# Intermediate stores moved to GpSimd's queue, and the opening's loads and first feature tile put in another order

## The chip, the cores and the metric
One core of one Trainium2 chip runs the whole program. The metric is the device time of one execution in microseconds. The engines are named as in the profile: PE (TensorE), DVE (VectorE), ACT (ScalarE), POOL (GpSimd) and SP (SyncE, which here only issues DMAs; its issue rows are marked SPq).

## The reference
Two layers of a trunk over 512 latent tokens and 256 context tokens of width 1024. Cut to what matters:
```python
for i in range(2):
    mod_l = silu(c) @ w_ada[i] + b_ada[i]          # shift, scale, gate
    mod_c = silu(c_ctx) @ w_ada[i] + b_ada[i]
    h_l = x * (1 + sc_l) + sh_l                    # 512 x 1024
    h_c = cx * (1 + sc_c) + sh_c                   # 256 x 1024
    parts = split(h @ w_in)                        # SSD | MLA | retention, with gates
    ssd = rms_norm(scan(conv5(xbc), softplus(dt + bias)) * silu(z))
    mla = softmax(q k^T) v * silu(gate)            # 8 heads, low-rank q and kv
    ret = head_norm(scan(q, k, v)) * silu(gate)    # 4 heads
    x = layer_norm(ALPHA * x + g * (concat(ssd, mla, ret) @ w_out))
return x                                           # latents only
```
Context tokens read only context; the scans run in both directions. All is fp32.

## The kernel before
Features lie on the 128 partitions and the 768 tokens on the columns: 0 to 255 context, 256 to 767 latent. Each fp32 product is done as three matmuls of split operands (`mm3`: hi with hi, hi with lo, lo with hi). `split` makes the parts: ScalarE casts hi, VectorE subtracts it for lo. So each weight tile costs a load (`wr`), a cast (`wh`) and a subtraction (`wl`) before TensorE can use it; `wslot` takes the common slots, two for `wr`, three each for `wh` and `wl`. `pslot` is the same in a slot of a stage's own pool.

`load` is a DMA from SyncE's queue, and before the change every DMA goes through it, stores as well. Much is stored to DRAM and loaded again later, often in another layout: the decay sums (`cum`, from the tile `ct`, back as `cf`), the convolved x (`xs`), the scan's outputs (`y`), MLA's inputs and operands (`cq`, `ckv`, `g`, `qh`, `kn`, `v`), retention's (`rq`, `rk`, `rv`, `rg`), the mixer's outputs (`m`), and both residual streams (`a`, `x`).

`start` is the opening. Sixteen tiles of the modulation weights (`ar`, in pairs k and k+8 for shift and scale of feature tile k) give matmuls `pr`; ScalarE copies the result (`rows`), TensorE turns it (`pm`), VectorE adds the bias (`mod`). `make_h0` loads feature tile k of x, scales and shifts it in place and splits it (`hh`, `hl`). Three weight tiles (one of 48 columns, which holds dt, and two of the convolution's inputs B and C) are then multiplied with it: matmuls `p` (latent columns) and `c` (context), 18 for each k, summed over the eight k.

Then the dt stage: `ms` is copied out, transposed (`pt`), goes through a softplus written out on VectorE, and ends in the cumulative sums `ct`, stored as `cum`. The tile `ct` shares its two buffers with `cv`, the result of the convolution, so the first convolutions (`cv<-xpad,cw`) must wait until the two stores of `cum` have read them. Behind that come the convolutions, the SSD scan with other projections (`pj`) put in between as filler, retention, MLA, and the output projection. In MLA a pair of heads ends with a chain through DRAM (`mla_head`): the denominators `den` are stored (`dd`), loaded again spread over 128 partitions (`dc`), inverted on VectorE, stored (`de`), loaded as broadcast rows (`den`), and multiplied with `num`; `den` has one buffer. This happens three times in each layer.

The order on each engine is fixed before the run by a scheduler that goes by the order of the code and by priorities (`high_priority`, which `wslot` asks for from its seventh tile on). Every engine executes in its order.

Of the kernel before, what the change touches and what calls it, by code (L numbers as in the profile page):

```python
# [18 lines left out]
KD = 8  # L19
NCTX = 256  # L20
# [68 lines left out]
class Trunk:  # L89
# [7 lines left out]
    def load(self, out, in_):  # L97
        return self.nc.sync.dma_start(out=out, in_=in_)

    def mm(self, out, lhsT, rhs, start=True, stop=True, **k):  # L100
        return self.nc.tensor.matmul(out, lhsT=lhsT, rhs=rhs, start=start, stop=stop, **k)  # L101
# [54 lines left out]

    def pslot(self, P, src, n):
        raw = P.tile([128, 1024], F32, tag="pwr", name="pwr", bufs=1)
        self.load(raw[:, :n], src)
        hi = P.tile([128, 1024], F32R, tag="pwh", name="pwh", bufs=1)  # L160
        lo = P.tile([128, 1024], F32R, tag="pwl", name="pwl", bufs=1)
        self.split(hi[:, :n], lo[:, :n], raw[:, :n])
        return hi, lo
# [40 lines left out]
    def store(self, dst, ps, gate=False):  # L204
        with self.tc.high_priority():
            st = self.sp.tile([128, T], F32, tag="st", name="st", bufs=3)
            for src, a, b in ps:
                if gate:
                    self.act(st[:, a:b], src, AF.Tanh, scale=0.5)
                    self.stt(st[:, a:b], st[:, a:b], 1.0, src, ALU.add, ALU.mult)  # L210
                else:
                    self.copy(st[:, a:b], src)
            self.load(dst[:, ps[-1][1]:T], st[:, ps[-1][1]:T])

# [93 lines left out]
    def start(self, P):  # L308

        tiles = ((M_T, 48), (B_T, 128), (B_T + 2, 128))  # L310
        lat = [self.acc.tile([128, 512], F32, tag="acc", name="p0") for _ in tiles]
        cx = [self.ps("cx", "c0", 3) for _ in tiles]
        ws = []
        for k in range(KD):
            for j in (0, 1) if k == 0 else (k + 1,):
                if j < KD:
                    self.ada(0, (j, j + 8), P)
            self.make_h0(P, k)
            if not ws:
                for t, m in tiles:  # L320
                    ws.append([x[:, :8 * m].rearrange("p (k c) -> p k c", k=8)
                               for x in self.wslot(self.A["win"][0, t][:, :8 * m], 8 * m)])
            for ps, a, b in ((lat, NCTX, T), (cx, 0, NCTX)):
                for p, (hi, lo), (t, m) in zip(ps, ws, tiles):
                    self.mm3(p[:m, 0:b - a], [(hi[:, k, :], lo[:, k, :], self.hh[k][:, a:b], self.hl[k][:, a:b])],
                             k == 0, k == KD - 1)
        self.first = []
        for pl, pc, (t, m) in zip(lat, cx, tiles):
            st = self.sp.tile([128, T], F32, tag="st", name="c0s", bufs=3)
            self.copy(st[:m, 0:NCTX], pc[:m, 0:NCTX])  # L330
            self.first.append([(pl[:m], NCTX, T), (st[:m, 0:NCTX], 0, NCTX)])
# [99 lines left out]
    def dt_stage(self):  # L431
# [26 lines left out]
        self.load(D["kr"], ms[0:32, :])  # L458
        pt = self.ps("tr", "pt", 2)
# [49 lines left out]
        for d, m in ((0, self.mf), (1, self.mb)):  # L509
            pa = self.ps("tr", "pa", 2)  # L510
            pb = self.ps("tr", "pb", 2)
            for c in range(NCH):
                o = pa[0:16, c * 128:(c + 1) * 128] if c < 4 else pb[0:16, (c - 4) * 128:(c - 3) * 128]
                self.mm(o, la[:, d, c, :], m)
            ct = S.tile([16, T], F32, tag="cv", name="ct", bufs=2)
            self.copy(ct[:, 0:512], pa[0:16, :])
            self.copy(ct[:, 512:T], pb[0:16, 0:256])
            self.load(D["cum"][d].rearrange("c h i -> h c i"), ct.rearrange("h (c i) -> h c i", i=128))
        self.cw = S.tile([128, 72], F32, name="cw")
# [31 lines left out]
    def xbc(self, g):  # L551
        nc, S, l, D = self.nc, self.S, self.l, self.D
        self.uB = S.tile([128, XC], F32, name="uB")
        self.uC = S.tile([128, XC], F32, name="uC")
        self.conv(B_T + g, self.uB)
        self.conv(B_T + 2 + g, self.uC)
        self.bt = S.tile([128, NCH, 128], F32, name="bt")
        self.xt = S.tile([128, NCH, 512], F32, name="xt")
        self.trans(self.uB, self.bt)
        for t in range(4):  # L560
            u = self.conv(X_T + g * 4 + t)
            if self.ctx:
                self.load(D["xs"][g * 4 + t][:, 0:NCTX], u[:, 0:NCTX])
            self.load(D["xs"][g * 4 + t][:, NCTX:T], u[:, 260:XC])
            self.trans(u, self.xt[:, :, t * 128:(t + 1) * 128])
# [41 lines left out]
    def ssd_y(self, c, g, hf, hb):  # L607
# [49 lines left out]
        self.tt(yv, cv[hs[0][0]], py, ALU.add)  # L657
        self.load(D["y"][g][:, :, c * 128:(c + 1) * 128].rearrange("t p i -> p t i"), ys)


    def ret_v(self):
        l = self.l
        for n in range(2):
            sl = [self.wslot(self.A["win"][l, RV_T + n * 2 + j]) for j in range(2)]
            sl = [(a.rearrange("p (k c) -> p k c", k=4), b.rearrange("p (k c) -> p k c", k=4)) for a, b in sl]
            for c in range(NCH):
# [4 lines left out]
                with self.tc.high_priority():  # L671
# [9 lines left out]
                    self.load(self.D["rv"][:, c, n * 256:(n + 1) * 256], st)  # L681

# [144 lines left out]
    def ret_y(self, P, c0, q, kk, v, Dm, ef, hs):  # L827
# [44 lines left out]
        for s in range(2):  # L872
# [6 lines left out]
            for pr in range(2):  # L879
                self.load(D["m"][4 + pr * 2 + s][:, cs], gt[:, s, pr])  # L880


    def mla_prep(self, P):
# [46 lines left out]
        nc.vector.tensor_copy(ko[:, 0:NCTX], kr[:, 0:NCTX])  # L930
        self.load(D["krr"], ko)

# [4 lines left out]
        for p in range(4):  # L937
            st = P.tile([128, T], F32, tag="st", name="st", bufs=2)
            for a, b in ((NCTX, T), (0, NCTX)):
# [4 lines left out]
                self.tt(st[:, a:b], ps[:, 0:b - a], krb[:, a:b], ALU.mult)  # L944
            self.load(D["kn"][p], st)
        wvh, wvl = v3(wv[0], 2), v3(wv[1], 2)
        for c in range(NCH):
# [4 lines left out]
            self.act(st, ps, AF.Copy, scale=ky[:, c:c + 1])  # L952
            self.load(D["v"][:, c, :], st)

        qh, ql, qrb, _ = normed(D["cq"], 3, P_QN, 384, ctx)
        bl = ([(0, NCTX)] if ctx else []) + [(NCTX, T)]
        for s in (2, 0, 1):
            w = self.pslot(P, self.A["wuq"][l, s], 768)
            wh, wl = v3(w[0][:, 0:768], 3), v3(w[1][:, 0:768], 3)
            for j in range(2):  # L960
# [13 lines left out]
                if ti < 4:  # L974
                    for s2 in range(2):
                        self.load(D["qh"][ti * 2 + s2][0:64, lo:], st[64 * s2:64 * s2 + 64, lo:])
                else:
                    for s2 in range(4):
                        self.load(D["qh"][(ti - 4) * 4 + s2][64:96, lo:], st[32 * s2:32 * s2 + 32, lo:])

# [62 lines left out]
    def mla_head(self, P, h):  # L1043
# [47 lines left out]
        self.load(D["m"][p][:, lo:], num[:, lo:])  # L1091

# [46 lines left out]
    def out_s(self, t):  # L1139
# [11 lines left out]
        else:  # L1151
# [4 lines left out]
            self.stt(x[:, lo:], x[:, lo:], self.ag[:, 8 + t:9 + t], y[:, lo:], ALU.add, ALU.add)  # L1156
        self.load(self.D["a"][t][:, lo:], x[:, lo:])

# [87 lines left out]
    def ln(self, P, X, a, b, qsum, xsum):  # L1246
# [32 lines left out]
        for t in range(8):  # L1279
# [5 lines left out]
            if a >= NCTX:  # L1285

                self.load(D["x"][t][:, a:b], X[t])
        if a >= NCTX:
            rr = P.tile([1, NLAT], F32, name="rr")
            self.copy(rr, pb[0:1, :])  # L1290
            self.load(self.rrd, rr)

# [90 lines left out]
```

## Time and profile before

| | |
|---|---|
| median of 3 runs | 1487.89 us (1486.96 to 1489.88) |
| the profiled execution | 1487.2 us, its span 1485.4 us |
| mean granted clock of TensorE | 0.982 |
| busy share of the span | PE 95%, DVE 73%, ACT 47%, POOL 2% |
| instructions of GpSimd | 31, none of them a DMA |
| DMA | 225.66 MB, 152 GB/s in the mean |

The span runs from the first to the last instruction that the profiler recorded; the rest of an execution lies around it. Times in the trace count from the span's start. The busy share of PE is an average over stages in which different things limit, and matmuls overlap in a pipeline, so a PE that is busy is not always at its peak.

### The profile page before, as it was taken

The numbers are of one execution on the slowest core, as the hardware profiler recorded it, in microseconds if no ns is written. First come the engines' busy times: TensorE is split into PE (matmuls) and PEld (weight loads), VectorE is DVE, ScalarE is ACT, GpSimd is POOL, SyncE is SP. The second block draws the span as 40 slices with busy tenths as digits, with TensorE's granted clock in tenths as the row PEclk, the third lists the DMA queues.
The fourth block names the chain that finished last, engine by engine and source line by source line (L and its number), as shares of the span: only waits on it lengthen the run. The fifth ranks groups of instructions, "written<-read, shape, count | busy, mean of one in ns | idle before, by whom it ended". The sixth has DMA issues, their size and how long they took to land. (4 is left out here: it accounts for less than half of the span.)

```text
span 1485.4 us, 23355 instructions
## 1 busy us (share of the span) xinstructions
PE 1418.2 (95%) x8660; PEld 1158.9 (78%) x8660; DVE 1084.7 (73%) x2132; ACT 693.0 (47%) x1376; POOL 22.5 (2%) x31
## 2 busy tenths in 40 slices
PE   6999999999999999999999799999999999989996
PEld 4787789778888878777788688789878887767665
DVE  3599894995485657678745858998697678678858
ACT  2346743662232434477721245565363335347743
POOL 0000000000000001000001000000000000000010
PEclk9999999999999999999999899999999999999998
DMA  8336543457724746724242222353257455563241
GB/s 335 137 101 178 184 171 107 158 183 256 256 72 157 254 160 182 240 65 137 89 156 71 91 88 87 129 135 114 86 171 226 173 188 189 196 202 98 67 128 57
DMA packets 110155, 225.66 MB, mean 152 GB/s; under 512 B 13581, under 2 KB 42381, under 8 KB 109786
## 3 DMA queue, kind: packets, MB, share of 16 engines
q1 hardware_dynamic: 110042, 224.17, 46.2%
q8 instruction: 68, 1.11, 0.3%
q14 instruction: 45, 0.37, 0.1%
HBM read 173.93 MB, written 50.20 MB: 151 GB/s over the span
## 5 line engine op out<-in xcount | busy, mean ns | idle before, releaser
L101 PE MATMUL pj<-hh,wh 128*128 128x512 f32 (+1 forms) x984 | 354.6, 361 | 2.0 <-ACT hh L115 1.6
L101 PE MATMUL pj<-hh,wl 128*128 128x512 f32 (+1 forms) x984 | 352.7, 359 | 0.0
L101 PE MATMUL pj<-hl,wh 128*128 128x512 f32 (+1 forms) x984 | 349.9, 356 | 0.0
L122 ACT CAST wh<-wr 128x1024 fp32r<-128x1024 f32 (+1 forms) x116 | 120.3, 1039 | 207.1 <-PE pj L101 94.0
L101 PEld LDWEIGHTS pj<-hh,wh 128*128 128x128 f32 x984 | 186.7, 190 | 34.0 <-issue 9.3
L101 PEld LDWEIGHTS pj<-hh,wl 128*128 128x128 f32 x984 | 186.4, 190 | 29.4 <-issue 7.0
L101 PEld LDWEIGHTS pj<-hl,wh 128*128 128x128 f32 x984 | 186.7, 190 | 29.0 <-issue 6.4
L104 DVE TENSOR_TENSOR wl<-wr,wh 128x1024 fp32r<-128x1024 f32 (+1 forms) x116 | 142.4, 1227 | 75.8 <-ACT wh L122 75.0
L104 DVE TENSOR_TENSOR pel<-pe,peh 128x512 fp32r<-128x512 f32 (+1 forms) x112 | 71.6, 648 | 35.8 <-ACT peh L115 35.3
L107 DVE SCALAR_TENSOR_TENSOR cv<-xpad,cw,cv 128x772 f32<-128x772 f32 (+1 forms) x96 | 92.2, 994 | 0.2
L115 ACT ACTIVATE pe<-psc 128x512 f32<-128x512 f32 (+1 forms) x112 | 63.7, 569 | 55.6 <-PE psc L101 46.7
L1035 DVE TENSOR_REDUCE nm<-pmx 128x1 fp32r<-128x768 f32 (+1 forms) x80 | 67.6, 845 | 15.8 <-PE pmx L101 14.6
L101 PE MATMUL po<-sh,wh 128*128 128x512 f32 (+1 forms) x192 | 69.4, 364 | 4.2 <-DVE oy L107 4.2
L101 PE MATMUL po<-sl,wh 128*128 128x512 f32 (+1 forms) x192 | 69.5, 363 | 1.7 <-DVE sl L107 1.7
L115 ACT ACTIVATE ce<-cf 64x512 f32<-64x512 f32 (+1 forms) x80 | 46.9, 586 | 49.6 <-DMA cf<-cum 48.9
L101 PE MATMUL po<-sh,wl 128*128 128x512 f32 (+1 forms) x192 | 68.9, 360 | 0.0
L115 ACT ACTIVATE tm<-sf,dt 128x128 f32<-128x128 f32 x160 | 52.5, 390 | 30.2 <-DVE sf L104 30.2
L115 ACT ACTIVATE peh<-psc 128x512 fp32r<-128x512 f32 (+1 forms) x112 | 63.6, 568 | 0.2
L115 ACT ACTIVATE arg<-arg,ncb 128x128 f32<-128x128 f32 x160 | 54.9, 393 | 4.2 <-DVE arg L107 3.8
L101 PE MATMUL pv<-wl,hh 128*128 128x256 f32 x192 | 54.7, 285 | 0.3 <-DVE wl L104 0.3
L101 PE MATMUL po<-mr,wh 128*128 128x256 f32 (+1 forms) x216 | 54.8, 339 | 0.0
L101 PE MATMUL pv<-wh,hl 128*128 128x256 f32 x192 | 54.5, 284 | 0.0
(330 smaller groups left out, 2952.2 us busy)
## 6 DMA issues: line engine op xcount, KB each, us to landing
wr<-in_win SPq DMA_DIRECT2D x82, 512.0 KB, 3.8
ar<-in_wada SPq DMA_DIRECT2D x48, 512.0 KB, 7.0
cf<-cum SPq DMA_DIRECT2D x80, 256.0 KB, 4.6
wr<-in_wout SPq DMA_DIRECT2D x32, 512.0 KB, 4.0
y<-ys SPq DMA_DIRECT2D x20, 256.0 KB, 2.6
xs<-th SPq DMA_DIRECT2D x16, 256.0 KB, 2.1
x<-in_xT SPq DMA_DIRECT2D x8, 384.0 KB, 8.7
rv<-stv SPq DMA_DIRECT2D x24, 128.0 KB, 2.6
```

Of the source, the lines that this page charges most:

```text
L101: return self.nc.tensor.matmul(out, lhsT=lhsT, rhs=rhs, start=start, stop=stop, **k)
L104: return self.nc.vector.tensor_tensor(out, a, b, op=op)
L107: return self.nc.vector.scalar_tensor_tensor(out, in0=a, scalar=s, in1=b, op0=op0, op1=op1)
L115: return self.nc.scalar.activation(out, in_, f, **k)
L122: self.nc.scalar.copy(hi, raw)
L1035: nc.vector.tensor_reduce(nm[:, i:i + 1], p1[:, 0:n], axis=AX.X, op=ALU.max, negate=True)
```

## The change
Two things are edited. A new helper `save` issues a DMA from GpSimd's queue, and 231 stores use it in place of `load`; the final stores of `out` and all loads stay on SyncE's. And `start` is written in another order: for the first feature tile the modulation pair 0, then x, then the three weight tiles, of which the small one takes a slot of its own through `pslot`; only then the pair for the next feature tile, and from there on always one pair ahead.
```diff
+    def save(self, out, in_):
+        return self.nc.gpsimd.dma_start(out=out, in_=in_)
...
-    def pslot(self, P, src, n):
-        raw = P.tile([128, 1024], F32, tag="pwr", name="pwr", bufs=1)
+    def pslot(self, P, src, n, size=1024):
+        raw = P.tile([128, size], F32, tag="pwr", name="pwr", bufs=1)
...
         for k in range(KD):
-            for j in (0, 1) if k == 0 else (k + 1,):
-                if j < KD:
-                    self.ada(0, (j, j + 8), P)
-            self.make_h0(P, k)
-            if not ws:
+            if k == 0:
+                self.ada(0, (0, 8), P)
+                self.make_h0(P, 0)
                 for t, m in tiles:
-                    ws.append([x[:, :8 * m].rearrange("p (k c) -> p k c", k=8)
-                               for x in self.wslot(self.A["win"][0, t][:, :8 * m], 8 * m)])
+                    w = (self.wslot(self.A["win"][0, t]) if m == 128 else
+                         self.pslot(P, self.A["win"][0, t][:, :8 * m], 8 * m, 8 * m))
+                    ws.append([x[:, :8 * m].rearrange("p (k c) -> p k c", k=8) for x in w])
+            if k + 1 < KD:
+                self.ada(0, (k + 1, k + 9), P)
+            if k:
+                self.make_h0(P, k)
...
-            self.load(D["cum"][d].rearrange("c h i -> h c i"), ct.rearrange("h (c i) -> h c i", i=128))
+            self.save(D["cum"][d].rearrange("c h i -> h c i"), ct.rearrange("h (c i) -> h c i", i=128))
...
-            self.load(d1[i:i + 1, :], den[64 * i:64 * i + 1, lo:])
+            self.save(d1[i:i + 1, :], den[64 * i:64 * i + 1, lo:])
...
-        self.load(fl(d2), dc)
+        self.save(fl(d2), dc)
```
The other stores are edited in the same way.

Three places show what this does to the engines' orders. The first is SyncE's queue at the start of the program, behind three small loads of constants (`ar` are modulation weights, `x` feature tiles, `wr` and `pwr` the projection's weights; `x2` and the like is a count).
```order
+L98 DMA ar<-in_wada 128x1024 x2
+L98 DMA x_144<-in_xT 128x768
+L98 DMA pwr<-in_win 128x384
+L98 DMA wr<-in_win 128x1024 x2
 L98 DMA ar<-in_wada 128x1024 x4
-L98 DMA x_171<-in_xT 128x768
-L98 DMA wr<-in_win 128x384
-L98 DMA wr<-in_win 128x1024
-L98 DMA ar<-in_wada 128x1024
-L98 DMA wr<-in_win 128x1024
-L98 DMA ar<-in_wada 128x1024
 L98 DMA x_240<-in_xT 128x768
```

The first feature tile and the weights now stand behind two modulation tiles instead of four, and the second weight tile of full size no longer behind a later `ar`.

The second is TensorE at the end of the opening. Before, behind the next-to-last projections of the last feature tile:
```order
L101 MATMUL c_116<-hl_7_104,wh 128x256
L101 MATMUL c_116<-hh_7_96,wl 128x256
L462 MATMUL pt<-K,ms 128x48 x6
L101 MATMUL pj<-hh_0_89,wh 128x512
L101 MATMUL pj<-hl_0_97,wh 128x512
L101 MATMUL pj<-hh_0_89,wh 128x256
```

and after, where these rows begin one `pj` behind the opening's last matmul `c`:
```order
L105 MATMUL pj<-hl_0_97,wh 128x512
L105 MATMUL pj<-hh_0_89,wl 128x512
L105 MATMUL pj<-hh_1_90,wh 128x512
L105 MATMUL pj<-hl_1_98,wh 128x512
L105 MATMUL pj<-hh_1_90,wl 128x512
L105 MATMUL pj<-hh_2_91,wh 128x512
L105 MATMUL pj<-hl_2_99,wh 128x512
L105 MATMUL pj<-hh_2_91,wl 128x512
L105 MATMUL pj<-hh_3_92,wh 128x512
L105 MATMUL pj<-hl_3_100,wh 128x512
L105 MATMUL pj<-hh_3_92,wl 128x512
L469 MATMUL pt<-K,ms 128x48 x6
```

Twelve projection matmuls `pj`, counting the one ahead of these rows, now stand between the opening and the six transposes `pt`, which stood ahead of all of them.

The third is GpSimd from its last constant at the program's start on, after the change:
```order
L1378 MEMSET const-uint8-127 128x1
L1386 UNCONDITIONAL_BRANCH
L102 DMA kr_557<-ms 32x768
L102 DMA cum_558<-ct 16x6x128 x2
L102 DMA xs_0_559<-th 128x256
L102 DMA xs_0_559<-th 128x512
L102 DMA xs_0_560<-th 128x256
L102 DMA xs_0_560<-th 128x512
L102 DMA rk_0_580<-st 128x768
```

Before, none of these stores stands there: they stand in SyncE's order, among the loads.

## Rows read from the trace of the kernel before

**Rows 1.** The page, part 1: busy us, share of the span, instructions.
```profile
PE 1418.2 (95%) x8660; PEld 1158.9 (78%) x8660; DVE 1084.7 (73%) x2132; ACT 693.0 (47%) x1376; POOL 22.5 (2%) x31
```

**Rows 2.** Waits of PE: us in total, times, longest us.
```profile
PE ptr L572 <- DVE th L107: 3.2, 2, 1.7
...
PE pq L101 <- ACT stv L115: 1.7, 1, 1.7
...
PE pvv L101 <- ACT stv L115: 1.3, 1, 1.3
```

**Rows 3.** Windows: length, busy us by engine, PEclk (granted clock), DMA share, GB/s.
```profile
17.00:45.00 28.00, 26.49 (x256) 19.31 (x254) 12.32 (x25) 6.28 (x10) 0.00 (x0) 0.94 1.01 393
60.00:62.00 2.00, 2.00 (x7) 1.49 (x6) 1.97 (x5) 0.08 (x2) 0.00 (x0) 0.50 0.26 76
76.00:232.00 156.00, 154.30 (x1049) 129.58 (x1048) 144.77 (x266) 90.65 (x212) 0.00 (x0) 1.00 0.50 157
```

**Rows 4.** Timeline of the opening: start us, us, engine, instruction, idle before.
```profile
6.92 1.08 PE L101 MATMUL pr<-ar,sil 128*32 128x128 f32 x16 [6.92 <-DMA ar<-in_wada]
...
10.64 0.35 DVE L112 TENSOR_SCALAR mod<-pm,pc 128x2 f32<-128x2 f32 x2 [6.12 <-PE pm L101]
...
13.81 0.86 DVE L112 TENSOR_SCALAR x<-x,mod 128x512 f32<-128x512 f32 x2
...
15.59 0.66 PE L101 MATMUL p<-hh,wh 128*48 128x512 f32 x1 [2.08 <-ACT hh L122]
...
25.48 1.25 PE L101 MATMUL p<-hh,wh 128*48 128x512 f32 x3 [0.97 <-ACT hh L122]
...
30.32 0.85 PE L101 MATMUL pr<-ar,sil 128*32 128x128 f32 x22
```

**Rows 5.** Timeline of the opening, SyncE's DMA issues (SPq).
```profile
6.23 0.57 SPq L98 DMA_DIRECT2D ar<-in_wada  x1
15.16 0.33 SPq L98 DMA_DIRECT2D wr<-in_win  x1
```

**Rows 6.** Timeline of PE at the opening's end.
```profile
58.23 0.57 PE L462 MATMUL pt<-K,ms 48*128 48x48 f32 x6 [1.60 <-ACT ms L118]
59.17 0.50 PE L101 MATMUL pj<-hh,wh 128*128 128x512 f32 x1 [0.38 <-ACT wh L122]
59.51 0.39 PE L101 MATMUL pj<-hl,wh 128*128 128x512 f32 x1
59.74 0.28 PE L101 MATMUL pj<-hh,wh 128*128 128x256 f32 x1
```

**Rows 7.** Waits in 76 to 232 us, of VectorE.
```profile
DVE wl L104 <- ACT wh L122: 5.2, 5, 2.7
```

**Rows 8.** Timeline, 74 to 77 us: the store of cum, and the first convolution.
```profile
74.30 2.20 SPq L98 DMA_DIRECT2D cum<-ct  x2
...
76.17 0.68 DVE L112 TENSOR_SCALAR cv<-xpad,cw 128x772 f32<-128x772 f32 x1 [2.00 <-ACT ct L118]
```

**Rows 9.** Timeline, 1355 to 1367 us: one chain of MLA's denominators.
```profile
1355.58 0.64 SPq L98 DMA_DIRECT2D dc<-dd  x1
...
1359.73 0.19 DVE L1085 RECIPROCAL dc<-dc 128x8 f32<-128x8 f32 x1
...
1361.38 1.10 SPq L98 DMA_DIRECT2D den<-de  x2
...
1366.16 0.68 DVE L107 SCALAR_TENSOR_TENSOR num<-num,den 128x512 f32<-128x512 f32 x1
```

**Rows 10.** DMA issues: count, KB each, median us from issue to landing.
```profile
v<-stv SPq DMA_DIRECT2D x12, 256.0 KB, 5.9
...
den<-de SPq DMA_DIRECT2D x6, 128.0 KB, 2.8
...
dc<-dd SPq DMA_DIRECT2D x3, 4.0 KB, 3.1
```

**Rows 11.** GpSimd's dearest group: busy us, mean ns.
```profile
L1214 POOL TENSOR_TENSOR lxs<-lxs,la 128x512 f32<-128x512 f32 x4 | 6.0, 1508 | 12.8 <-issue 10.3 <-DVE la L107 2.4
```

More of the change, by code (lines that the diff above doesn't have):

```diff
@@ L155, in wslot @@
         return hi, lo
-    def pslot(self, P, src, n):
-        raw = P.tile([128, 1024], F32, tag="pwr", name="pwr", bufs=1)
+    def pslot(self, P, src, n, size=1024):
+        raw = P.tile([128, size], F32, tag="pwr", name="pwr", bufs=1)
         self.load(raw[:, :n], src)
-        hi = P.tile([128, 1024], F32R, tag="pwh", name="pwh", bufs=1)
-        lo = P.tile([128, 1024], F32R, tag="pwl", name="pwl", bufs=1)
+        hi = P.tile([128, size], F32R, tag="pwh", name="pwh", bufs=1)
+        lo = P.tile([128, size], F32R, tag="pwl", name="pwl", bufs=1)
         self.split(hi[:, :n], lo[:, :n], raw[:, :n])
@@ L212, in store @@
                     self.copy(st[:, a:b], src)
-            self.load(dst[:, ps[-1][1]:T], st[:, ps[-1][1]:T])
+            self.save(dst[:, ps[-1][1]:T], st[:, ps[-1][1]:T])
     def run(self):
@@ L457, in dt_stage @@
                 self.padded[t] = self.pad(self.pre[t])
-        self.load(D["kr"], ms[0:32, :])
+        self.save(D["kr"], ms[0:32, :])
         pt = self.ps("tr", "pt", 2)
@@ L562, in xbc @@
             if self.ctx:
-                self.load(D["xs"][g * 4 + t][:, 0:NCTX], u[:, 0:NCTX])
-            self.load(D["xs"][g * 4 + t][:, NCTX:T], u[:, 260:XC])
+                self.save(D["xs"][g * 4 + t][:, 0:NCTX], u[:, 0:NCTX])
+            self.save(D["xs"][g * 4 + t][:, NCTX:T], u[:, 260:XC])
             self.trans(u, self.xt[:, :, t * 128:(t + 1) * 128])
@@ L657, in ssd_y @@
         self.tt(yv, cv[hs[0][0]], py, ALU.add)
-        self.load(D["y"][g][:, :, c * 128:(c + 1) * 128].rearrange("t p i -> p t i"), ys)
+        self.save(D["y"][g][:, :, c * 128:(c + 1) * 128].rearrange("t p i -> p t i"), ys)
     def ret_v(self):
@@ L680, in ret_v @@
                                  bias=vm[:, h:h + 1])
-                    self.load(self.D["rv"][:, c, n * 256:(n + 1) * 256], st)
+                    self.save(self.D["rv"][:, c, n * 256:(n + 1) * 256], st)
     def blocks(self):
@@ L879, in ret_y @@
             for pr in range(2):
-                self.load(D["m"][4 + pr * 2 + s][:, cs], gt[:, s, pr])
+                self.save(D["m"][4 + pr * 2 + s][:, cs], gt[:, s, pr])
     def mla_prep(self, P):
@@ L930, in mla_prep @@
         nc.vector.tensor_copy(ko[:, 0:NCTX], kr[:, 0:NCTX])
-        self.load(D["krr"], ko)
+        self.save(D["krr"], ko)
         wk = self.pslot(P, self.A["wukv"][l, 0], 1024)
@@ L944, in mla_prep @@
                 self.tt(st[:, a:b], ps[:, 0:b - a], krb[:, a:b], ALU.mult)
-            self.load(D["kn"][p], st)
+            self.save(D["kn"][p], st)
         wvh, wvl = v3(wv[0], 2), v3(wv[1], 2)
@@ L952, in mla_prep @@
             self.act(st, ps, AF.Copy, scale=ky[:, c:c + 1])
-            self.load(D["v"][:, c, :], st)
+            self.save(D["v"][:, c, :], st)
         qh, ql, qrb, _ = normed(D["cq"], 3, P_QN, 384, ctx)
@@ L975, in mla_prep @@
                     for s2 in range(2):
-                        self.load(D["qh"][ti * 2 + s2][0:64, lo:], st[64 * s2:64 * s2 + 64, lo:])
+                        self.save(D["qh"][ti * 2 + s2][0:64, lo:], st[64 * s2:64 * s2 + 64, lo:])
                 else:
                     for s2 in range(4):
-                        self.load(D["qh"][(ti - 4) * 4 + s2][64:96, lo:], st[32 * s2:32 * s2 + 32, lo:])
+                        self.save(D["qh"][(ti - 4) * 4 + s2][64:96, lo:], st[32 * s2:32 * s2 + 32, lo:])
     def mla(self, P):
@@ L1090, in mla_head @@
         self.tt(num[:, lo:], num[:, lo:], gt[:, lo:], ALU.mult)
-        self.load(D["m"][p][:, lo:], num[:, lo:])
+        self.save(D["m"][p][:, lo:], num[:, lo:])
     def mla_last(self, P):
@@ L1156, in out_s @@
             self.stt(x[:, lo:], x[:, lo:], self.ag[:, 8 + t:9 + t], y[:, lo:], ALU.add, ALU.add)
-        self.load(self.D["a"][t][:, lo:], x[:, lo:])
+        self.save(self.D["a"][t][:, lo:], x[:, lo:])
     def out_m(self, R, P):
@@ L1285, in ln @@
             if a >= NCTX:
-                self.load(D["x"][t][:, a:b], X[t])
+                self.save(D["x"][t][:, a:b], X[t])
         if a >= NCTX:
@@ L1290, in ln @@
             self.copy(rr, pb[0:1, :])
-            self.load(self.rrd, rr)
+            self.save(self.rrd, rr)
 INS = ["xT", "cT", "wada", "win", "wuq", "wukv", "wout", "pc", "cpack", "rope"]
```

## The prediction
> **What bounds the kernel now.** I read the page first. TensorE is busy for 95% of the span [rows 1], so whatever moves the end must shorten its idle time or its slow-clock time. The waits by engine then say where the idle time has a releaser, and of those that this change can reach there are few: transposes that wait for VectorE (3.2 us), and two projections of the MLA preparation that wait for ScalarE's staging tile stv (1.7 and 1.3) [rows 2]. None names a store. The windows give the stages [rows 3]: in 17 to 45 us the DMA engines are full (share 1.01, 393 GB/s); in 76 to 232 us TensorE has 154.30 of 156 us and VectorE 144.77, so there two engines are nearly full at once, and an engine that runs ahead gains only if the other follows. The reader is to see three places: the opening, its end at 56 to 60 us, and the long stage behind it.
>
> **The opening.** In it the first projection of feature tile 0 starts at 15.59 us, although the first modulation weights fed TensorE at 6.92 [rows 4]. What lies between is order: VectorE has the scale of feature tile 0 ready at 10.64 + 0.35, but the two products with x come at 13.81, behind the second pair of modulation columns; from there through ScalarE's hi cast to the matmul it is 1.78. SyncE's rows show the second fault: after its load at 6.23 it issues nothing until 15.16, because the third weight tile finds no free slot and waits for VectorE's split [rows 5]; that is a hole in the loads of 8.4 us less what was still in flight.
>
> After the change VectorE's product with x stands right behind the first modulation. Worked out: 10.99 us (mod done), if x0 has landed. It is fifth behind the two modulation tiles now: two of 512 KB and one of 384 KB are 1.44 MB, 3.7 us at the 393 GB/s of that window [rows 3]; the first tile fed TensorE at 6.92, so x0 lands about 2.3 us later, 9.3. Then the same 1.78: first projection at 12.8, **2.8 us earlier**.
>
> For feature tile 1 two things must be there. The loads in the new order up to x1 are 192 KB + 2 x 512 KB (weights), 4 x 512 KB and 384 KB, 3.74 MB or 9.5 us at that rate: 9.3 + 9.5 = 18.8. TensorE must do 18 matmuls of tile 0 (25.48 to 30.32 for those of tile 1 [rows 4]: 4.84), 64 modulation matmuls (16 took 1.08 at 6.92, right after idling; 64 would be 4.3 at that pace and 2.2 at twice it; I take 2.2, since TensorE will not have idled just before, and 0.9 for the handovers through ScalarE): 12.8 + 4.84 + 2.2 + 0.9 = 20.7. The later one counts. Then the scale, 0.35, the 1.78 again and a handover of 0.3: 23.1 against 25.48, **2.4 us earlier** (bounds 0.8 and 2.8). From there on the pace per tile is TensorE's own, before as after, so the opening ends 2.4 us earlier.
>
> **Its end.** Before, TensorE then idled 1.60 us until ScalarE had copied ms for the transposes pt, and 0.38 for the weight cast [rows 6], and the granted clock in 60 to 62 us was 0.50, its lower level (1.2 GHz), after that idling [rows 3]. In the changed order twelve pj matmuls stand between the last opening projection and pt, and their weight tile is split early, since the opening now holds only two of the common slots. So 2.0 us go, and, if the clock does not fall, also half of its low stretch: 1.0 for these two us, and 1.7 if it lasts half as long again and more. Together 2.0 to 3.7. TensorE enters the next stage **4.4 to 6.1 us ahead**.
>
> **What VectorE lets through.** It is the other full engine there. Its start on the convolutions does not move by as much: pt comes only 1.2 us earlier (2.4 and the gap of 1.60, less twelve matmuls at 0.23, from one start at 59.51 to the next at 59.74 [rows 6]), the softplus chain behind it is VectorE's own work, and the first convolution reuses the tile ct, so it waits until cum is stored: SyncE issues that at 74.30, and VectorE starts at 76.17, having waited 2.00 [rows 8]. This store moves to GpSimd. What a store costs from there no row shows, since GpSimd issues none now. Nearest rows from both sides: SyncE's issue of one transfer takes 0.33 [rows 5]; GpSimd's own dearest instruction 1.51 [rows 11]. Call the extra delay of a stored result d. From below it is 0 or less, for the stv stores take 5.9 us to land behind loads on SyncE's queue where dd to dc takes 3.1 [rows 10], so another queue can also help; from above I take 2, a little over GpSimd's row. I use **d = 1**, between, nearer GpSimd's own rows as it is GpSimd that works. So VectorE starts its convolutions at the same time as before (1.2 earlier, 1 later).
>
> VectorE gains in that stage only where it waited for TensorE or ScalarE behind TensorE: 5.2 us for the weights' hi casts [rows 7], which wait for slots that TensorE frees; with smaller waits besides I take 6 as the bound. Against it, the changed order puts some five more projection matmuls, 1.2 to 1.4 us, ahead of the places where TensorE needs VectorE. From the lead of 4.4 to 6.1, less those matmuls and under this bound, I take **4 us** gained at 232 (bounds 0 and 6). The transposes' wait for th [rows 2], up to 1.7 at once and one of the two at the end of this stage, shows that VectorE, not TensorE, decides there; that is why I don't pass on the whole lead.
>
> **The other 228 stores.** (231 less the three of the stage above, kr and cum.) SyncE's 0.33 for each is 75 us of its time, but none of the waits is on SyncE, so that saving is worth nothing in itself. Where stores free a tile that ScalarE needs (stv, 1.7 and 1.3 [rows 2]) a store that lands sooner gives up to 3.0. Where a load reads back what was stored, d is added: cum of layer 1 (+1), and six chains in MLA, den stored, dc loaded, reciprocal, stored, den loaded, num multiplied. Their slack [rows 9, 10]: dc issued at 1355.58 lands 3.1 later, 1358.7, and is used at 1359.73, so 1.0; den issued last at about 1362 lands 2.8 later, about 1364.8, used at 1366.16, so 1.4 to 1.5. With d = 1 the first store costs nothing; the second stays within 1.5. GpSimd's own few operations [rows 11] now stand behind stores that wait for their data; they were hidden behind TensorE's work at the layer's end, and without that cover four of them are 6 us, inside the upper bound. Net 0 (bounds -3 and +8).
>
> **Sum.** 1487.2 (the profiled execution's own time, span 1485.4 and 1.8 around it) - 4 + 0 = 1483.2. The median of the runs is 1487.89, 0.7 above that execution; forecast **1483.8**.
>
> **A rule against it.** VectorE, which in the long stage is busy for 144.77 of 156 us [rows 3], seldom leaves a moment in which nothing of its own runs beside a store of GpSimd's. The Trainium skill, SBUF — State Buffer, section "SBUF: two separate sides", says that the descriptors of a DMA from GpSimd's queue are written by GpSimd, that VectorE locks it out of a shared port while it runs an operation in a two-port mode, and, a section further ("A bandwidth-pool intuition that's wrong"), that a DMA of 0.62 us took 3.1 so. No run here shows it. By the page's difference d would be an estimated 2.5 and the forecast some 1501; by the rows d is 1.
>
> **Rivals.**
> *VectorE eats it all (0.22).* In 76 to 232 VectorE is full, its start is bound to the cum store, and the waits for hi casts may come back later. For it: 144.77 of 156 us. Against it: it did wait 5.2 us for casts. Then 0 to 2 us are left: 1485.5 to 1488.5, no change.
> *Stores late in chains (0.18), slower.* One mechanism, d, at cum and in the six chains. Price: 2(d-1) for the two cum places beyond what I counted, and for each chain what passes its slack, (d-1.0) + (d-1.5) on VectorE, which stalls in order, TensorE's pel behind it. At d = 2: 2 + 6 x 1.5 = 11, so 1483.8 + 11 = 1495. It decides the sign against the 4 us of gain at d of about 1.55 (1 + 6 x 0.6 = 4.7), and is measurably slower at about 1.75. For it: VectorE has no idle time there to take it up. Against: GpSimd is nearly idle (2%, 31 instructions [rows 1]). The rule above leads here.
> *More comes (0.13).* SyncE's loads no longer stand behind stores that wait for results, the stv waits go (3.0), the clock stays up at the opening's end, and the whole lead of 6.1 passes: 1487.9 - 6 - 3 = 1479, with less of other waits down to 1475.
> *As forecast (0.46).* 1480.5 to 1485, its own range.
> The rest, 0.01, is for what I don't see.
>
> **How the numbers follow.** About 0.2% is what a measurement of this kernel can tell from no change: under 1484.9 is faster, over 1490.9 slower. Faster: 0.46 less 0.03 for its upper end, and 0.13: 0.56. Same: 0.22 + 0.03 + 0.01, 0.26. Slower 0.18. The range must reach into the case of late stores up to 1492 and down to 1475.5; some 0.16 above and 0.03 below stay out.
>
> **What would show it.** In the profile after: the first p matmul near 12.8 us and that of feature tile 1 near 23.1; SyncE's issue row without the hole of 6.8 to 15.2; no idle time before pt, and a granted clock of 1.00 in 58 to 62; the first convolution on VectorE still at about 76; the transpose wait near 232 still there but 4 us earlier. For the stores: cum landing within 3 us of its issue (now VectorE starts 1.9 behind it), dd to dc within 1 us of its 3.1, and no new wait of VectorE for dc or den. The forecast is wrong if VectorE's convolutions start 2 us or more later or earlier, if RECIPROCAL waits for dc, or if pq and pvv wait longer for stv than 1.7 and 1.3.

## The result and the profile after

The changed kernel took 1498.16 us (median of 4 runs, 1497.09 to 1500.91) against 1488.89 for the kernel before (4 runs, 1486.96 to 1491.09). The ratio is 1.0069 with a 95% interval of 1.0046 to 1.0093: slower by 0.7%, where 0.3% faster was forecast. The profiled execution took 1498.86 us, its span is 1497.1, the mean granted clock 0.975 (0.982 before).

The page's busy times, to be held against [rows 1]:
```profile
PE 1421.7 (95%) x8660; PEld 1163.3 (78%) x8660; DVE 1084.7 (72%) x2132; ACT 693.1 (46%) x1376; POOL 151.0 (10%) x262
```
TensorE's and VectorE's work is the same. GpSimd went from 22.5 to 151.0 us, for here the 231 issues of stores count as busy. Of the 11.7 us of longer span TensorE is busy 3.5 us more with the same matmuls, and idle 8.2 us more.

The opening, PE and DVE rows of the timeline, against [rows 4]:
```profile
11.47 0.34 DVE L116 TENSOR_SCALAR mod<-pm,pc 128x2 f32<-128x2 f32 x2 [7.16 <-PE pm L105]
...
13.64 0.66 PE L105 MATMUL p<-hh,pwh 128*48 128x512 f32 x1 [2.21 <-ACT hh L126]
...
24.82 0.44 PE L105 MATMUL p<-hh,pwh 128*48 128x512 f32 x1 [1.52 <-ACT hh L126]
```
The first projection comes at 13.64 for 15.59, that of feature tile 1 at 24.82 for 25.48. The windows of the same stages (length, busy us by engine, granted clock, DMA share, GB/s), against [rows 3]:
```profile
14.00:17.00 3.00, 2.93 (x9) 1.61 (x8) 2.93 (x3) 1.48 (x2) 0.00 (x0) 1.00 1.02 409
17.00:45.00 28.00, 25.53 (x296) 18.94 (x296) 11.70 (x29) 5.76 (x11) 0.00 (x0) 1.00 0.93 365
58.00:62.00 4.00, 4.00 (x25) 3.52 (x24) 3.97 (x9) 1.58 (x3) 0.00 (x0) 1.00 0.44 136
76.00:232.00 156.00, 153.00 (x1035) 128.31 (x1034) 145.35 (x271) 93.37 (x218) 16.72 (x28) 0.99 0.52 158
```
The hole in the loads (14 to 17 us) is filled, and the clock at the opening's end is 1.00. The store of cum and the first convolution, against [rows 8]:
```profile
72.06 0.56 POOL L102 DMA_DIRECT2D cum<-ct  x1 [14.51 <-ACT ct L122]
...
74.21 0.68 DVE L116 TENSOR_SCALAR cv<-xpad,cw 128x772 f32<-128x772 f32 x1 [2.56 <-DMA cum<-ct]
```
VectorE starts 2.15 us behind the store's issue (1.87 before) and 2.0 us earlier than before. Up to here the change does what was expected of it.

Where it goes then is seen from single TensorE instructions that stand in both kernels at the same place of the work. Their rows before (a wait in brackets ends at the row's start):
```profile
234.10 0.88 PE L572 MATMUL ptr<-K,th 128*128 128x128 f32 x6 [1.73 <-DVE th L107]
...
846.12 2.07 PE L101 MATMUL prs<-K,rs_y 128*128 128x128 f32 x8 [4.72 <-DVE rs_y L107]
...
1019.87 0.85 PE L572 MATMUL ptr<-K,th 128*128 128x128 f32 x6 [1.44 <-DVE th L107]
...
1229.77 1.50 PE L101 MATMUL pcol<-ones,nx 128*128 128x1 f32 x12
```
and after:
```profile
230.08 0.83 PE L579 MATMUL ptr<-K,th 128*128 128x128 f32 x6
...
850.29 2.07 PE L105 MATMUL prs<-K,rs_y 128*128 128x128 f32 x8 [4.71 <-DVE rs_y L111]
...
1023.44 0.84 PE L579 MATMUL ptr<-K,th 128*128 128x128 f32 x6 [1.57 <-DVE th L111]
...
1238.30 1.96 PE L105 MATMUL pcol<-ones,nx 128*128 128x1 f32 x11 [3.37 <-DVE nx L108]
```
The distances are -4.0 us at the transposes near 232, +4.2 at the end of layer 0, +3.6 at layer 1's transposes, +8.5 at pcol, +11.7 at the end (the spans). So the lead was 4 us, as forecast; some 8 were lost between 232 and 850, 5 between 1023 and 1238, and 3 behind that. Of the 8, 3.7 are lost before the first pcol of layer 0 (493.43 before, 493.09 after), where no wait of TensorE is over 1.2 us, and 3.8 from there to the second pcol (536.43 and 539.94).

Two places have a long new wait. The first, in this last stretch, all engines of the changed kernel near 520 us (POOL rows are issues of stores):
```profile
518.11 0.33 SPq L98 DMA_DIRECT2D pwr<-in_wuq  x1
...
518.55 0.36 SPq L98 DMA_DIRECT2D ar<-in_wada  x1
...
518.66 0.54 POOL L102 DMA_DIRECT2D kn<-st  x1 [5.19 <-DVE st L108]
...
525.44 0.69 ACT L119 ACTIVATE stv<-pvv,rya 128x512 f32<-128x512 f32 x1 [4.85 <-DMA kn<-st]
...
526.18 0.80 PE L105 MATMUL pvv<-pwh,nh 128*128 128x512 f32 x1 [3.06 <-ACT stv L119]
```
TensorE waits 3.06 us for ScalarE's copy into the staging tile stv; that copy waited 4.85 us for the store of kn, whose tile shares the two staging buffers. The store was issued at 518.66, half a microsecond behind a load of 384 KB and at the time of one of 512 KB that SyncE issued, and ScalarE went on at 525.44, 6.8 us later.

So late a store is not new. In the kernel before, where SyncE issues it, at the same place:
```profile
523.53 0.89 SPq L98 DMA_DIRECT2D ar<-in_wada  x2
525.61 1.33 SPq L98 DMA_DIRECT2D v<-stv  x2
...
532.18 1.31 ACT L115 ACTIVATE stv<-pvv,rya 128x512 f32<-128x512 f32 x2 [1.78 <-DMA v<-stv]
...
532.93 0.50 PE L101 MATMUL pq<-nh,pwh 128*128 128x512 f32 x1 [1.70 <-ACT stv L115]
```
The store of v went out at 525.61, 2.1 us behind two loads of 512 KB, and ScalarE went on 6.6 us later; TensorE waited 1.70 us. After the change the wait is longer, not the landing. The second place, SyncE's issues in layer 1:
```profile
1222.09 0.32 SPq L98 DMA_DIRECT2D zy<-y  x1
1223.53 0.32 SPq L98 DMA_DIRECT2D zx<-xs  x1
...
1224.94 0.52 SPq L98 DMA_DIRECT2D nx<-ckv  x1
...
1229.23 0.38 SPq L98 DMA_DIRECT2D nx<-ckv  x1
```
and before:
```profile
1218.76 0.90 SPq L98 DMA_DIRECT2D nx<-ckv  x2
```
Before, the two loads of nx went out together, at 1218.76. Now one more pair of zy and zx stands ahead of them, and a weight load between them: they go out at 1224.94 and 1229.23, 2.6 and 6.4 us late beyond the 3.6 of layer 1's start (the second one was issued at 1219.28 before). TensorE's pcol waits 3.37 us for what is made of them, and then the granted clock is low. The windows around both places in the changed kernel (columns as above):
```profile
500.00:560.00 60.00, 56.05 (x328) 47.17 (x328) 35.36 (x70) 18.94 (x28) 9.41 (x18) 0.94 0.51 173
1170.00:1260.00 90.00, 83.02 (x433) 68.25 (x432) 66.82 (x147) 33.75 (x50) 4.81 (x9) 0.91 0.45 140
```

Median times from issue to landing of stores, from SyncE in the kernel before, against [rows 10]:
```profile
y<-ys SPq DMA_DIRECT2D x20, 256.0 KB, 2.6
...
kn<-st SPq DMA_DIRECT2D x8, 384.0 KB, 2.3
```
and now from GpSimd:
```profile
y<-ys POOLq DMA_DIRECT2D x20, 256.0 KB, 3.0
...
kn<-st POOLq DMA_DIRECT2D x8, 384.0 KB, 3.0
v<-stv POOLq DMA_DIRECT2D x12, 256.0 KB, 2.3
```
By the medians half of the groups land 0.4 to 1.0 us later, a few later still, as rg (7.2 for 6.0), and a few no later. But before, the trace tells the landing of only some of the stores. Of v it tells three of twelve (2.6, 5.9 and 6.5 us), and the 5.9 is their median; now it tells all twelve, and four of these take 4.1 us or more.

### The profile page after: what moved, and what is told of

Same layout as the page of the kernel before. It is cut to its first block, busy times and chain, and to the rows that moved or that the text cites. A ratio compares the mean times of both kernels' runs of the same rounds, so it can differ in the third digit from the quotient of the medians.

```text
span 1497.1 us, 23525 instructions
## 1 busy us (share of the span) xinstructions
PE 1421.7 (95%) x8660; PEld 1163.3 (78%) x8660; DVE 1084.7 (72%) x2132; ACT 693.1 (46%) x1376; POOL 151.0 (10%) x262
## 4 chain that ended last, share of the span: by engine, by line
PE 62%; issue 19%; DMA 7%; DVE 5%; ACT 5%; POOL 2%; SPq 0%; POOLq 0%; ACTq 0%; DVEq 0%
PE pj L105 25%; PE po L105 7%; PE ppv L105 4%; PE psc L105 4%; PE pv L105 3%; PE pstate L105 2%; DMA cf<-cum 2%; PE pq L105 2%; PE pin L105 2%; PE pr L105 2%; PE py L105 1%; PE pmx L105 1%; PE p L105 1%; PE pry L105 1%; DMA mraw<-m 1%
## 5 line engine op out<-in xcount | busy, mean ns | idle before, releaser
L1042 DVE TENSOR_REDUCE nm<-pmx 128x1 fp32r<-128x768 f32 (+1 forms) x80 | 67.7, 846 | 12.8 <-PE pmx L105 12.0
```

The lines of the kernel that those rows point to most:

```text
L1042: nc.vector.tensor_reduce(nm[:, i:i + 1], p1[:, 0:n], axis=AX.X, op=ALU.max, negate=True)
```

## The experiments

All were timed on chips on which the kernel before had a median of 1491.5 to 1492.0 us, so each is given as a ratio of the runs to those of before, with its 95% interval. The waits and clocks come from one profiled execution of each kernel, and executions of one kernel spread by up to 1.1%.

**The two parts apart.** First the opening alone, `save` being `load` again:
```diff
     def save(self, out, in_):
-        return self.nc.gpsimd.dma_start(out=out, in_=in_)
+        return self.nc.sync.dma_start(out=out, in_=in_)
```


> The new opening with all stores issued by SyncE as before. In the profile after the change TensorE was about 4.3 us ahead of before at 232 us and some 11.7 us behind at the end. If the opening is a gain and the stores alone are the loss (both theories below say so), this kernel takes 1483 to 1486 us, with no new wait after 300 us. If the lead of the opening is lost by itself in later stages, 1487 to 1490 us.

Measured: 1485.63 us (12 runs), ratio 0.9966 (0.9949 to 0.9983). Then the stores alone, with the loop of the old `start`:
```diff
-            if k == 0:
-                self.ada(0, (0, 8), P)
...
+            for j in (0, 1) if k == 0 else (k + 1,):
+                if j < KD:
+                    self.ada(0, (j, j + 8), P)
+            self.make_h0(P, k)
```


> The old opening with the 231 stores from GpSimd's queue. If the two parts add up, 1500 to 1504 us, that is some 4 us over the changed kernel. If the loss comes of the two together (the lead shifts later work into worse places), 1488 to 1494 us.

Measured: 1508.91 us (6 runs), ratio 1.0122 (1.0090 to 1.0155), above the range of either theory. The opening is a gain of 0.34%, the stores a loss of over 1%, and the two multiply as they should: 1.0069 / 0.9966 = 1.0103 lies in the second interval. The opening alone beats both kernels.

**The two places.** The preparation's stores back on SyncE (krr, kn, v and qh, one line shown):
```diff
-            self.save(D["v"][:, c, :], st)
+            self.load(D["v"][:, c, :], st)
```


> The changed kernel with only the stores of the MLA preparation (krr, kn, v, qh) back on SyncE. Theory of late stores: a store from GpSimd's queue lands later by itself, and in the preparation ScalarE waits for it to free the staging tile, so most of what layers lose there, 5 to 8 us, comes back: 1490 to 1493 us. Theory of order: the loss near 1235 us comes from the loads of nx standing behind more loads of zy and zx on SyncE, which this does not mend; only the 3 us wait of pvv near 523 us and its slow clock come back: 1493 to 1497 us.

Measured: 1.0084 (1.0056 to 1.0112). A miss of both theories: nothing came back. And nx of layer 1 ahead:
```diff
-                self.load(x[:, a0:], src[t][:, a0:])
+                with (self.tc.high_priority() if l and nt == 2 else ExitStack()):
+                    self.load(x[:, a0:], src[t][:, a0:])
```


> The changed kernel with the two loads of nx from ckv in layer 1 given priority, so that they stand ahead of one weight load and the rope tables on SyncE. Theory of order: the wait of pcol for nx near 1235 us and the slow clock behind it shrink, 4 to 9 us come back: 1489 to 1494 us. Theory of late stores: nothing changes, 1497 to 1499 us.

Measured: 1.0032 (1.0010 to 1.0053). By the medians about a third of the loss against the opening's 0.9966 came back, but the interval overlaps that of the changed kernel. The wait of pcol fell from 3.4 to 2.2 us; that profile is of the shortest of the 12 executions (1487.89 us, the median is 1495.68).

**Which stores.** Four kernels move only some of the stores, all with the new opening. Each keeps the others' lines as `load`. First all but retention's result:
```diff
-                self.save(D["m"][4 + pr * 2 + s][:, cs], gt[:, s, pr])
+                self.load(D["m"][4 + pr * 2 + s][:, cs], gt[:, s, pr])
```


> The changed kernel with only the 20 stores of retention's result (m from rgt) back on SyncE. In the order this gives, the two loads of nx from ckv in layer 1 stand behind 11 loads of zy and zx as before, not behind 13. Theory of order: the wait of pcol for nx and the long slow clock behind it go, as in the run with nx first or better: a ratio to the kernel before of 0.998 to 1.003. Theory of late stores: 211 of 231 stores still come from GpSimd, so nearly nothing changes against the changed kernel: 1.005 to 1.009.

Measured: 1.0054 (1.0035 to 1.0073). Against the theory of order. The first load of nx still goes out only at 1224.13, pcol and po still wait 1.4 and 2.5 us there, and the wait near 520 is untouched at 3.3.

> The new opening with only the stores of the projections' staging tiles, of rv and of retention's result on GpSimd; cum, xs, y, the MLA preparation, the denominators' chains and the outputs on SyncE. The order has nx behind 13 loads of zy and zx. Theory of order: the loss near 1235 us shows here too, ratio 0.999 to 1.004, against 0.997 for the opening alone. Theory of late stores: no store of a chain is moved, so the opening's gain stays: 0.995 to 0.998.

Measured: 1.0064 (1.0039 to 1.0088). The price is there with no chain's store moved, but it is higher than the range of either theory.

> The new opening with only the stores that are read back in chains on GpSimd: kr, cum, xs and y of the SSD part, the denominators' dd and de and their result m. Nx stands behind 11 loads as before. Theory of late stores: the price of the six chains and of cum shows, ratio 1.000 to 1.005. Theory of order: the ratio stays near the opening's own, 0.995 to 0.999.

Measured: 0.9985 (0.9965 to 1.0004). The chains, on which my slower rival rested, cost some 0.2% by the medians, with intervals that overlap.

> The new opening with only the stores of the MLA preparation (krr, kn, v, qh) on GpSimd. If the wait of pvv near 523 us for ScalarE's staging tile, 3.1 us with a slow clock behind it in the changed kernel, comes of these stores meeting loads of SyncE that now run ahead, it shows here, in both layers, ratio 0.998 to 1.002. If it came of other parts of the change, the ratio stays at 0.995 to 0.998.

Measured: 1.0073 (1.0050 to 1.0096). Neither range held it: these stores alone, 0.7% over before, are 1.07% over the opening's own.

> The changed kernel with both the stores of the MLA preparation and those of retention's result back on SyncE, all others (SSD, projections, rv, the denominators' chains, the outputs: over half of the 231) on GpSimd. Nx stands behind 11 loads. If the loss is made at these two places (the preparation's staging tile, whose stores meet loads that run ahead, and the loads of nx behind zy and zx), it is gone: ratio to the kernel before 0.996 to 1.000. If any large move of stores costs its per cent wherever it is made (each of four subsets did), 1.004 to 1.008.

Measured: 0.9984 (0.9963 to 1.0005). With both groups left on SyncE the loss is gone although over half of the stores are on GpSimd. The preparation's stores alone (1.0073), or retention's with those of the projections (1.0064), are enough to lose about a per cent against the opening, which fits that mending one group gave nothing. The waits of TensorE in the profiles go with the groups (longest wait in us; "ahead" counts the loads of zy and zx of layer 1 in front of the first and second nx):

| kernel | preparation's stores | ahead | pq or pvv for stv, 500 to 540 | pcol for nx, 1220 to 1250 | ratio |
|---|---|---|---|---|---|
| opening alone | SyncE | 11, 11 | 1.4 | 0.3 | 0.9966 |
| chains moved | SyncE | 11, 11 | 1.2 | 2.0 | 0.9985 |
| neither | SyncE | 11, 11 | none | 1.0 | 0.9984 |
| nx first | GpSimd | 13, 13 | 3.4 | 2.2 | 1.0032 |
| retention's back | GpSimd | 11, 11 | 3.3 | 1.4 | 1.0054 |
| projections and retention's | SyncE | 13, 13 | none | 3.5 | 1.0064 |
| changed kernel | GpSimd | 13, 13 | 3.1 | 3.4 | 1.0069 |
| preparation's | GpSimd | 11, 11 | 4.1 | 0.4 | 1.0073 |
| preparation's back | SyncE | 13, 13 | none | 3.3 | 1.0084 |
| stores alone | GpSimd | 13, 13 | 3.4 | 3.0 | 1.0122 |

In this table every kernel with a wait of 3 us or more at either place is slower than before, and every one without is not. That the waits go with the loss does not show that they make it. The profile of the preparation's run ends 18.0 us behind that of the opening alone; 2.5 of them are lost between the two pcols of layer 0, where its wait of 4.1 is, and 9.3 between there and the first pdt (739.95, for 724.14 in the opening alone). TensorE's order in the two is the same only up to 505 us. And the run was 4.1 us behind at the first pcol (489.08 for 485.02), before its first store from GpSimd, at 496.75, so two profiles can differ by that much without the change.

**A third staging buffer.** In the preparation, five tiles share the tag:
```diff
-            st = P.tile([128, 512], F32, tag="st", name="stv5", bufs=2)
+            st = P.tile([128, 512], F32, tag="st", name="stv5", bufs=3)
```


> The run with only the preparation's stores on GpSimd (ratio 1.0073), and the staging tile of the preparation with three buffers for two. If the loss there is ScalarE and VectorE waiting for a store that stands behind loads, a third buffer covers most of it: no wait of pvv for stv over 1.5 us near 520 and 1273 us, ratio 0.997 to 1.002. If it comes of the changed order of matmuls, it stays: 1.005 to 1.009.

Measured: 1.0062 (1.0038 to 1.0086); the wait near 520 is still 3.6 us.

> The changed kernel with both mends: retention's result stored by SyncE, and three staging buffers in the preparation. With 211 stores on GpSimd; if these two places make the loss, ratio 0.996 to 1.001, against 1.0054 with the first mend alone. If late stores cost elsewhere, 1.003 to 1.006.

Measured: 1.0250 (1.0225 to 1.0274), the worst of all, with waits of only 2.7 and 1.3 us at the two places.

> The control of the third buffer: the opening alone, all stores on SyncE, three staging buffers. The waits of pq or pvv for stv (1.4 and 1.8 us with two buffers) go: ratio 0.994 to 0.997, against 0.9966 with two. If stv was not what held TensorE there, 0.996 to 0.998.

Measured: 1.0037 (1.0018 to 1.0056). The waits for stv did go, to 0.7 us and none, and the kernel is slower than before with no long wait at either place. The control shows why the other two say little: the third buffer alone, with nothing on GpSimd, costs 0.7% against the opening, and TensorE's order is another from 507 us on. Against its own control the preparation's move costs 0.25% here, with intervals that overlap. Inconclusive.

**The mechanism at each place.** No store on GpSimd, only the loads of zy and zx in layer 1 ahead:
```diff
-            self.load(y[:, lo:], D["y"][t // 4][t % 4][:, lo:])
-            self.load(x[:, lo:], D["xs"][t][:, lo:])
+            with (self.tc.high_priority() if l and t in (5, 6) else ExitStack()):
+                self.load(y[:, lo:], D["y"][t // 4][t % 4][:, lo:])
+                self.load(x[:, lo:], D["xs"][t][:, lo:])
```


> All stores on SyncE, with the new opening, and only the loads of zy and zx for the z tiles 5 and 6 of layer 1 given priority, so that nx of layer 1 stands behind 13 and 14 of them as in the changed kernel, instead of 11. Nothing of GpSimd is in it, and TensorE's order is that of the opening alone up to about 1180 us. If the place of nx on SyncE makes the loss there, pcol waits 2.5 us or more for nx near 1230 us, a slow clock follows, and the ratio goes from 0.9966 to 0.999 to 1.004. If the loss needs the late stores, no such wait and 0.995 to 0.998.

Measured: 0.9997 (0.9981 to 1.0013), inside the range of the order theory, though the wait has another name and the interval just overlaps that of the opening alone (0.9949 to 0.9983). SyncE and PE rows of this kernel:
```profile
1215.08 0.43 SPq L98 DMA_DIRECT2D nx<-ckv  x1
...
1217.12 0.37 SPq L98 DMA_DIRECT2D nx<-ckv  x1
...
1227.67 1.65 PE L105 MATMUL po<-sh,wh 128*128 128x512 f32 x3 [4.24 <-ACT sh L119]
```
Nx goes out at 1215.08 and 1217.12, apart; in the opening alone both at 1210.09 (0.90 us for two). ScalarE does nx first and sh behind it, so here po waits for sh, 4.24 us. The window behind it in this kernel and then in the opening alone:
```profile
1170.00:1240.00 70.00, 62.86 (x329) 52.70 (x328) 51.11 (x106) 27.70 (x40) 1.47 (x2) 0.88 0.55 172
```
```profile
1170.00:1240.00 70.00, 66.08 (x359) 54.42 (x359) 53.13 (x109) 27.36 (x40) 0.00 (x0) 0.98 0.53 170
```
0.88 for 0.98 in mean granted clock, and 62.86 for 66.08 us of TensorE busy. Part of this is only put off: at the end this profile is 2.2 us behind that of the opening alone (spans of 1484.9 and 1482.7).

The other place: the preparation's stores on GpSimd, and layer 1's modulation weights loaded as an eighth of each tile.
```diff
-            self.load(raw, self.A["wada"][l, j])
+            w = 1024 if P is not None else 128
+            self.load(raw[:, 0:w], self.A["wada"][l, j][:, 0:w])
...
-raw[:, k * 128:(k + 1) * 128],
+raw[:, k * 128 % w:k * 128 % w + 128],
```


> The run with only the preparation's stores on GpSimd, and the loads of layer 1's modulation weights (ar) cut to an eighth: each tile's first 128 columns serve all eight parts, so the modulation of layer 1 is another, with the same matmuls. If the wait of pvv for stv near 520 us (4.1 us, ratio 1.0073) comes of stores that land behind these 512 KB loads, it falls under 1.5 us and the ratio to 0.2 to 0.4% over that of the control with the same cut. If a store from GpSimd's queue is late by itself, the wait stays at 3 to 4 us and the distance to the control at 0.8 to 1.2%.

> The control: the new opening with all stores on SyncE and the same cut of layer 1's modulation loads. These loads were hidden, so the ratio stays near the opening's own, 0.994 to 0.998.

Measured: 0.9993 (0.9975 to 1.0011), and the control 0.9975 (0.9962 to 0.9988): 0.18% between them, with intervals that overlap, where the same move cost 1.07% with whole loads (1.0073 for 0.9966). The place with whole loads, all engines:
```profile
512.52 0.33 SPq L98 DMA_DIRECT2D ar<-in_wada  x1
...
513.66 0.33 SPq L98 DMA_DIRECT2D pwr<-in_wuq  x1
...
514.80 0.33 SPq L98 DMA_DIRECT2D wr<-in_wout  x1
...
516.25 0.33 SPq L98 DMA_DIRECT2D zy<-y  x1
...
516.57 0.54 POOL L102 DMA_DIRECT2D v<-stv  x1 [3.87 <-ACT stv L119]
516.67 0.38 SPq L98 DMA_DIRECT2D ar<-in_wada  x1
...
523.33 0.69 ACT L119 ACTIVATE stv<-pvv,rya 128x512 f32<-128x512 f32 x1 [5.17 <-DMA v<-stv]
...
524.07 0.80 PE L105 MATMUL pvv<-pwh,nh 128*128 128x512 f32 x1 [4.14 <-ACT stv L119]
```
Five loads of 384 or 512 KB go out between 512.52 and 516.67, the store of v at 516.57 in the midst of them, and ScalarE gets its buffer at 523.33: 6.8 us. With the cut loads:
```profile
517.70 0.33 SPq L98 DMA_DIRECT2D pwr<-in_wuq  x1
...
520.29 0.54 POOL L102 DMA_DIRECT2D v<-stv  x1 [3.55 <-ACT stv L119]
...
522.68 0.69 ACT L119 ACTIVATE stv<-pvv,rya 128x512 f32<-128x512 f32 x1 [1.52 <-DMA v<-stv]
```
One load is in flight, the store is issued at 520.29, the buffer is free at 522.68: 2.4 us, and TensorE does not wait there. The queue is the same in both, so a store from GpSimd is not late by itself; it is late beside loads, as SyncE's store of v was before (6.6 us). The cut also moves when these loads are issued, so both, their size and their time, may have a part in it. It gives TensorE another order as well, from 466 us on, so that the 1% itself comes of these loads is not shown.

## Why the prediction was wrong

**The opening, right in its sum.** Its first term was 12.8 us for the first projection; 13.64 was measured, since the second modulation tile fed TensorE at 9.39, 0.8 later than before; why, no row shows. Feature tile 1 came at 24.82 for 23.1, 0.7 us earlier than before, under my lower bound of 0.8. That the pace from there on is the same before as after was wrong too: the granted clock in 17 to 45 us was 1.00 for 0.94, and the last projection started at 54.19 for 56.34, 2.15 earlier where I had 2.4. That the two misses nearly cancel is luck. At the end of the opening there was no wait before pt and a clock of 1.00 in 58 to 62. At 232 us the lead was 4.0 us, as forecast (5.0 in the opening alone), and the opening alone takes 0.34% off, 5.1 us of 1491.6.

**VectorE's start, off by a size.** I held it in place: 1.2 earlier by pt, 1 later by d. pt came 1.09 earlier (57.14 for 58.23), and the store of cum landed 0.3 later by VectorE's row (2.15 for 1.87). But the store was also issued earlier than pt explains, for a split of a weight tile (1.23 us at 71.03 before) no longer stood ahead of it in VectorE's order. So VectorE started 2.0 us earlier, at the bound that I had named.

**The other 228 stores: the step that failed.** "Net 0 (bounds -3 and +8)" was a loss of 1.0%, 15 us, by the change's 1.0069 over the opening's 0.9966 (of all 231 stores). Two sentences in it fell. "None of the waits is on SyncE, so that saving is worth nothing in itself" took SyncE's order as costing and giving nothing; but a store that waits for its data there also holds back the loads behind it. Two rows of SyncE's waits before (us in total, times, longest us) were
```profile
SPq L98 <- DVE wl L104: 239.6, 66, 12.1
...
SPq L98 <- ACT stv L115: 62.6, 35, 5.0
```
and with the stores moved away it runs on until a slot stops it:
```profile
SPq L98 <- DVE wl L108: 409.2, 71, 29.8
```
Loads then go out at other times and in another order, as at nx. And "a store that lands sooner gives up to 3.0", for the tile stv, had the sign wrong: the longest wait for stv went from 1.7 to 3.1 us (pq and pvv, one of the signs that I had named). The 5.9 us of [rows 10] was a median of three landings; the late store of the row took 6.6 us before and 6.8 after, so nothing landed sooner where ScalarE waits. "None names a store" was a reading of TensorE's rows alone: ScalarE's row, one step back, names the store of v. How the 15 us divide is known only in part: the profile of the changed kernel is 14.4 us behind that of the opening alone, 8.1 of them at the first pcol of layer 0 already (493.09 for 485.02), 12.0 at the second (539.94 for 527.92), 13.8 at the end of layer 0 (850.29 for 836.53). In 234 to 495 us neither has a wait of TensorE over 1.2 us, but the mean granted clock is 0.98 for 1.00, by which some 5 us of the 7 lost there are slow clock; why it fell there stays open.

**The rivals.** *Stores late in chains* had the sign and nearly the time (1495), but not the place, so that was luck: the six chains and cum cost some 0.2%. RECIPROCAL did not wait for dc, and num waited 1.1 us at the longest for den (0.6 before). The rule behind it, in the Trainium skill's SBUF — State Buffer, section "SBUF: two separate sides", is that VectorE locks GpSimd out while it runs an operation in a two-port mode. Whether it ran such operations here no run shows; no sign of the rule was seen, for seven of the twelve stores of v landed in 2.3 us, and the late store's 6.8 us fell to 2.4 with smaller loads. What the runs agree with is the Trainium skill, DMA: Bandwidth & Descriptors, section "Issuing engines are not separate DMA queues": transfers from all queues share the same engines and interleave. It says that a second queue saves only issue time; here it also undid an order between loads and stores. *More comes* rested on loads no longer standing behind stores, which came true, and brought no gain.

**What the scheduler adds.** I compared orders only at the opening. The move of stores changed TensorE's order wherever it was tried, and two runs with nothing on GpSimd show what another order alone can do: zy and zx ahead cost 0.3% by the medians (0.9997 for 0.9966, the intervals just overlap), a third buffer, with the other order that came of it, 0.7%. So order is a rival for the whole loss, and no run holds it still while stores move. How much of the loss, in particular the wait of pnm near 612 us (3.1, before 1.7) and the losses behind 1240, belongs to order and how much to stores beside loads is left open; so is what the retention's stores do when moved without those of the projections, which was not tried. The low clock behind the waits differs between profiles too: behind pcol's 3.4 us the granted clock of the changed kernel is 0.50 from 1239 to 1256 us, behind the 2.2 us of the run with nx first it is back at 1.00 from 1236 us on.

## What to carry to other kernels

A store in the queue of the loads is also a brake on the loads behind it. Before moving stores to another queue, follow a wait one engine further back, to the store that frees a staging tile, and look for the loads in flight at that moment; the longest landing counts, and a median of three says little. Where a scheduler orders the instructions, compare the order of loads over the whole program, not at the edited place: by the medians, a load that slips behind two others in front of a critical stage cost as much here as the opening gave. And measure two edits apart: here one of them was worth 0.3% by itself.

## What the runs showed of the hardware that was not expected

The issue of most stores takes GpSimd 0.54 us (0.76 for the y tiles), against SyncE's 0.33 (0.37). A store of v freed its tile after 6.6 us from SyncE, and one of kn after 6.8 from GpSimd, with loads of 384 or 512 KB issued shortly before; with one load in flight a store of v from GpSimd did so after 2.4. Behind the two long waits TensorE's granted clock went to its lower level, 1.2 GHz: the mean is 0.94 in 500 to 560 us and 0.91 in 1170 to 1260 us of the changed kernel. In the opening alone the matching stretches, some 10 to 15 us earlier, read
```profile
490.00:550.00 60.00, 57.35 (x339) 47.53 (x338) 38.40 (x75) 22.87 (x34) 0.00 (x0) 1.00 0.53 175
1160.00:1245.00 85.00, 81.08 (x441) 66.83 (x441) 66.45 (x144) 32.30 (x47) 1.48 (x2) 0.98 0.49 156
```
that is 1.00 and 0.98. As an estimate by the means, (1 - 0.94) x 60 and (1 - 0.91) x 90, the slow clock there costs 3.6 and 8.1 us, more than the two waits themselves.
